# A hybrid encoder layer on one core: router logits from rows ahead of their norm, and the first tokens' branches inside the attention loop

## The chip, the cores and the metric

The kernel runs on one core of one Trainium2 chip as one program. The metric is the device time of one execution in microseconds; the number that counts is the median of several executions on the chip. Engines are named as in the profile: PE (TensorE matmul), PEld (its weight load), DVE (VectorE), ACT (ScalarE), POOL (GpSimd), SP (the queue that issues most DMAs).

## What is computed

One layer on 2048 tokens of width 1024, in float32. Cut to what matters here:

```python
h   = rmsnorm(x, norm1_g);  proj = h @ w_in          # RWKV columns | attention columns | two gates
y_rwkv = rwkv7_branch(...) @ w_rwkv_out              # group norm of the scan's output, bonus, gate
y_attn = dilated_attention_branch(...) @ w_attn_out  # 3 dilations, merged by their softmax sums
gates  = sigmoid(gate_logits)
x   = x + (gates[:, :, 0] * y_rwkv + gates[:, :, 1] * y_attn) @ w_out
h2  = rmsnorm(x, norm2_g)                            # x * rsqrt(mean(x * x) + eps) * norm2_g
grp_logits = h2 @ w_router_group  + b_router_group   # 4 groups, the best is taken
exp_logits = h2 @ w_router_expert + b_router_expert  # 32 experts, 2 of the 8 in that group
moe = sum over the two experts of  weight * ((silu(h2 @ w_gate[e]) * (h2 @ w_up[e])) @ w_down[e])
out = x + moe
```

## The kernel before

The program is one long unrolled sequence. Products that must be exact in float32 are made from a rounded part and the rest of it (`wh[:, 0]` and `wh[:, 1]`, the rest being "raw minus rounded", a subtraction), in three passes each.

1. *Projection, scan, dense products* (to about 1793 us). They leave the scan's output `y_d`, queries, keys and values `qkv_d` and gates `g_d` in DRAM.
2. *Attention* (lines 893 to 973): dilation groups `g` = 2, 1, 0, each with 16 windows of 128 tokens; group 0 goes by pairs of windows. A window transposes its q/k rows into PSUM under the tag `tq` (two buffers, L909), makes scores (L938, L940), exponentials (L947), transposes them (L953), multiplies with the values (L963) and stores `ob` to `o_d`. `parts_of_weights` loads and splits the weights of the next stage in between. Memory of this stage is the pool `at` and the PSUM pool `psC`; `stC.close()` (L1046) frees both.
3. *Preparation of the first 256 tokens*: constants (L975 to L987), then `rwkv(0, psC, "tq")` (L997): it loads the scan's output, norms it by head on DVE, adds the bonus on POOL (L1030, L1031), multiplies with the gate product (L1036, L1037) and turns the result with `split_T` (L988) into `YT[0]`. After `stC.close()` the pools `y5` and `psE` open, and `attn(0)` (L1124) loads the three groups' outputs `oc`, weights and adds them on DVE (L1133 to L1149) and turns them into `OT[0]`.
4. *Eight blocks `q` of 256 tokens* (L1223): eight calls of `merge` (gated sums, L1166 to L1173, with gates `tg` loaded at L1160 and L1161), then per tile `j` of 128 tokens two calls of `residual` (L1182, tag `px`). `norm2` (L1186) stores the row, squares it on ACT, takes the root on DVE (`rsqrt`, L105 to L110, small operations), and makes `h2` (L1194). `logits` (L1198) transposes `h2` (tag `th`, L1204), copies it on ACT (L1206) and multiplies with `wr` (L1209); L1212 adds the biases. `route` (L1064) picks group and experts on DVE, counts ranks with two matmuls (L1100, L1101, tag `pl`), and at last places tokens (L1117 to L1122). The odd tile's logits and the route of block `q` are a generator, `late`, that is advanced in block `q + 1`; so are `attn(q + 1)` and `rwkv(q + 1)`, as `nA` and `nR`, in block `q`. PSUM of this stage: `ab`, `t5` and `px` with two buffers each, `pl` and `th` with one.
5. *End of the route* (L1256 to L1279): experts are ordered by their counts; a matmul makes the tables `IDX1`, `IDX2`, `EOF` and the weights. `load_gu(0, G)` loads the first expert's weights and splits them (L1296 on ACT, L1297 with `eng`, here POOL).
6. *32 experts in that order*: rows fetched by POOL's indirect DMA (L1386), products (L1426, L1431, L1470), results added to the output by indirect DMA.

The order of instructions on each engine, and of DMAs on SP, is not that of the source. A planner orders them at build time: it takes what its own model finds ready, the earlier place in the source first, and gives out the buffers of each tag in that order. At run time every engine and queue is strictly in order. A pool's memory can be written when the last user of what lay there is done; the constants' pool `w5` and `yb`, and later the experts' `rw` and `sw`, lie on the same side of the memory.

## Time and profile before

| | us |
|---|---|
| median of 3 executions (lowest, highest) | 3318.16 (3314.29, 3323.53) |
| the profiled execution | 3319.97 |
| its span, first to last instruction | 3318.2 |
| PE / PEld / DVE / ACT / POOL busy, share of span | 91% / 74% / 67% / 46% / 17% |
| attention, first transposes to last output | 1793.5 to 2047.7 |
| from there to the first residual product | to 2086.0 |
| eight blocks, to the last residual product | to 2511.1 |
| route and first rows, to the first expert's first product | to 2556.9 |
| experts | to 3318.2 |

How to read the rows below. A row of a table by stretches gives the stretch, its length, then for PE, PEld, DVE, ACT and POOL the busy time in us and the number of instructions in it, then the granted TensorE clock as a share of full speed, the DMA engines' busy share and GB/s. A row of waits gives the engine, what it was about to do and its line, "<-" what it waited for, then the us in total, how often, and the longest. A row of the timeline gives start in us, duration of the merged group in us, engine, line, operation, written tile "<-" read tiles, shapes and the number of instructions; in brackets the idle time of that engine ahead of it and what ended it. A matmul of float32 takes two passes and shows as such in the durations.

### The profile page before, as it was taken

How to read it: one execution, taken by the hardware profiler on the slowest of the kernel's cores; microseconds unless marked ns; L12 is line 12 of the kernel's file. 1: busy time of each engine (PE TensorE's matmuls, PEld its weight loads, DVE VectorE, ACT ScalarE, POOL GpSimd, SP SyncE). 2: the span in 40 equal slices, each digit the busy share in tenths (PEclk: the TensorE clock that was granted, in tenths of full speed). 3: DMA queues.
4: the chain of work that ended last, by engine and by line, in shares of the span. 5: the costliest groups of instructions: out<-in, count | busy, mean ns of one | idle time of the engine just before them, and what ended most of it. 6: DMA issues, size and time to landing. Idle time of an engine off the chain costs nothing. (4 is left out here: it accounts for less than half of the span.)

```text
span 3318.2 us, 71986 instructions
## 1 busy us (share of the span) xinstructions
PE 3009.8 (91%) x29005; PEld 2449.2 (74%) x29005; DVE 2219.4 (67%) x4149; ACT 1538.3 (46%) x2946; POOL 563.3 (17%) x648
## 2 busy tenths in 40 slices
PE   6999978888989989998999987999996999999997
PEld 4788777668867787678877986877784667777775
DVE  6433367576867686749664876668764677788885
ACT  6633344453343434443524864111112666777764
POOL 0000012020202121202110001324233111222231
PEclk9999988999989999999999998999997999999998
DMA  7244365666545654554556554444333889999996
GB/s 277 80 124 147 112 223 182 216 206 201 159 150 187 196 181 147 172 187 156 167 175 192 177 171 140 127 137 135 129 114 124 295 298 333 339 336 340 328 308 198
DMA packets 361242, 652.75 MB, mean 197 GB/s; under 512 B 33741, under 2 KB 181917, under 8 KB 356674
## 3 DMA queue, kind: packets, MB, share of 16 engines
q1 hardware_dynamic: 338698, 599.74, 54.1%
q0 software_dynamic: 11104, 36.32, 4.4%
q10 hardware_dynamic: 11104, 12.06, 1.2%
q8 instruction: 229, 3.75, 0.5%
q14 instruction: 107, 0.88, 0.1%
HBM read 497.59 MB, written 153.16 MB: 196 GB/s over the span
## 5 line engine op out<-in xcount | busy, mean ns | idle before, releaser
L1297 DVE TENSOR_TENSOR wh<-raw,wh 128x1024 fp32r<-128x1024 f32 x376 | 442.4, 1221 | 78.6 <-ACT wh L1296 78.2
L724 PE MATMUL dn<-wh,hk 128*128 128x256 f32 x3456 | 472.4, 294 | 19.3 <-DVE wh L667 5.5
L724 PEld LDWEIGHTS dn<-wh,hk 128*128 128x128 f32 x3456 | 441.0, 198 | 38.5 <-issue 10.6
L1296 ACT ACTIVATE wh<-raw 128x1024 fp32r<-128x1024 f32 x384 | 387.0, 1053 | 140.6 <-DMA raw<-in_w_down_dram 61.0
L728 PE MATMUL dn<-hk,wh 128*128 128x512 f32 x1536 | 406.0, 412 | 27.2 <-DVE wh L667 10.1
L1426 PE MATMUL pgu<-wh,xT 128*128 128x512 f32 x1536 | 375.1, 401 | 0.2 <-ACT xT L1401 0.2
L728 PEld LDWEIGHTS dn<-hk,wh 128*128 128x128 f32 x1536 | 286.9, 194 | 103.3 <-ACT gs L738 12.1
L1426 PEld LDWEIGHTS pgu<-wh,xT 128*128 128x128 f32 x1536 | 286.1, 189 | 77.4 <-issue 6.1
L282 PE MATMUL pp<-hq,wh 128*128 128x512 f32 x1008 | 248.7, 399 | 1.4 <-ACT hq L218 1.1
L282 PEld LDWEIGHTS pp<-hq,wh 128*128 128x128 f32 x1008 | 188.1, 189 | 47.1 <-ACT hq L218 1.8
L1182 PE MATMUL px<-w,mT 128*128 128x512 f32 x768 | 198.7, 410 | 0.0
L1470 PE MATMUL py<-wh,hT 128*128 128x512 f32 x768 | 191.3, 401 | 0.5 <-ACT hT L1448 0.5
L484 POOL TENSOR_TENSOR t<-t,ld 128x512 f32<-128x512 f32 x32 | 53.7, 1677 | 806.9 <-DVE t L473 525.3
L1182 PEld LDWEIGHTS px<-w,mT 128*128 128x128 f32 x768 | 144.6, 191 | 37.3 <-issue 3.4
L1470 PEld LDWEIGHTS py<-wh,hT 128*128 128x128 f32 x768 | 140.4, 188 | 33.1 <-issue 1.2
L1362 POOL DMA_INDIRECT out_dram<-ys,IDX x49 | 102.5, 2092 | 303.7 <-issue 93.9
L738 ACT ACTIVATE gs<-dn,drv 128x512 f32<-128x512 f32 x64 | 75.8, 1184 | 128.4 <-PE dn L728 101.8
L1166 PE MATMUL ab<-yT,w 128*128 128x256 f32 x768 | 113.6, 292 | 7.5 <-DVE tg L1169 3.9
L1386 POOL DMA_INDIRECT xg<-h_d,IDX x49 | 73.0, 1489 | 276.8 <-PE tx L1400 155.8
L285 ACT ACTIVATE u<-pp 128x512 f32<-128x512 f32 x56 | 61.2, 1094 | 123.8 <-PE pp L282 98.6
L1166 PEld LDWEIGHTS ab<-yT,w 128*128 128x128 f32 x768 | 98.6, 191 | 12.9 <-DVE tg L1169 6.1
L423 ACT ACTIVATE uv<-pre 32x512 f32<-32x512 f32 x128 | 75.2, 588 | 59.6 <-PE pre L417 58.4
(416 smaller groups left out, 5454.8 us busy)
## 6 DMA issues: line engine op xcount, KB each, us to landing
wh<-wc_d SPq DMA_DIRECT2D x204, 512.0 KB
raw<-in_w_gate_dram SPq DMA_DIRECT2D x64, 1024.0 KB
raw<-in_w_up_dram SPq DMA_DIRECT2D x64, 1024.0 KB
raw<-in_w_down_dram SPq DMA_DIRECT2D x64, 1024.0 KB
wc_d<-wh SPq DMA_DIRECT2D x68, 512.0 KB
ld<-rkk_d SPq DMA_DIRECT2D x192, 128.0 KB
raw<-in_w_in_dram SPq DMA_DIRECT2D x82, 256.0 KB
g_d<-gs SPq DMA_DIRECT2D x64, 256.0 KB
```

The costliest lines, as they stand in the source:

```text
L282: PE.matmul(pp, whs[k // 4][:, a, k % 4], hq[q][k // 2][:, k % 2, b], start=n == 0, stop=n == 3 * KT - 1)
L423: S.activation(uv[p * 64:p * 64 + 32, s::2].rearrange("p s (h e n) -> p s h e n", e=2, n=N)[:, :, :, e], pa[o:o + 32], AF.Copy)
L724: PE.matmul(pp[e][:, j * 256:(j + 1) * 256], lhs(2 * e + j, hk, k, a), wk_[:, b], start=k + j + m == 0, stop=k + j + m == KT + 2, skip_gro ...
L728: PE.matmul(pp[e], wk_[:, a, e * 128:e * 128 + 128], hk[k // 2][:, k % 2, b], start=k + m == 0, stop=k + m == KT + 1)
L738: S.activation(natural(gs), by_residue(pp[e]), AF.Tanh, scale=0.5, bias=DP[:, 38 + ct:39 + ct])
L1166: PE.matmul(pa[:, e], wt[k][:, a, cs_], src[:, k, b], start=e + n == 0, stop=n == 3 * nk - 1, skip_group_check=True)
L1182: PE.matmul(px, mT[k // 4][:, k % 4, a, j * 128:(j + 1) * 128], wO[k][:, b, fs], start=n == 0, stop=n == 3 * KT - 1)
L1296: S.activation(wh[:, 0, ks], raw[:, ks], AF.Copy)
L1297: eng.tensor_tensor(wh[:, 1, ks], raw[:, ks], wh[:, 0, ks], op=OP.subtract)
L1362: G.indirect_dma_start(out=x2_d, out_offset=bass.IndirectOffsetOnAxis(ap=idx, axis=0), in_=src, in_offset=None, bounds_check=T - 1, oob_is ...
L1426: PE.matmul(pgu[n], xT[:, x_, 4 * a + k], wh[:, w_, k], start=a + k + m == 0, stop=a + k + m == 6)
L1470: PE.matmul(py[f], hT[:, x_, 2 * a + k], wh[:, w_, k, f * 512:(f + 1) * 512], start=a + k + m == 0, stop=a + k + m == 4)
```

## The change

Four things are done.

- The constants' loads, `split_T` and `rwkv` stand ahead of the attention loop. `wr` is multiplied with `norm2_g` (`g2T`) once. A new generator `attn0` makes the weighted sum of the first two tiles in buffers of `yb` (tags `y0`, `y1`, and small ones). `early`, the chain of `rwkv(0)` and `attn0`, is advanced once per window of group 0 from window 8 on. What is left behind `stC.close()` is `turn_o(0)`, the transposes and their split.
- `norm2` returns the root `r2`; `logits` transposes `xr` itself and puts `r2` into its last operation. Both halves are transposed and copied first (tag `t5`, two buffers; `th` is gone), then the 16 matmuls follow; `pl` has two buffers.
- `late` is advanced at other places: transposes of the odd tile after merge 3, its logit matmuls and the first part of the route after merge 7 and ahead of the residual, the ranks behind `residual(xr[0], mT, 0, 1)` as before, the placing of tokens behind the last residual. At the end the experts' order is worked out ahead of the last placing, in other buffers.
- `load_gu(0)` splits the first expert's weights on DVE, not POOL.

```diff
+    wr = mk(w5, [128, KT, 36], F32, "wr")
+    nc.sync.dma_start(wr[:, :, 0:4], w_router_group[0].rearrange("(k p) e -> p k e", p=128))
+    nc.sync.dma_start(wr[:, :, 4:36], w_router_expert[0].rearrange("(k p) e -> p k e", p=128))
+    g2T = mk(yb, [128, KT], F32, "bsum")
+    nc.sync.dma_start(g2T, norm2_g[0].rearrange("(k p) -> p k", p=128))
+    V.tensor_tensor(wr, wr, g2T[:, :, None].to_broadcast([128, KT, 36]), op=OP.mult)
...
+    def attn0():
+
+        for j in range(2):
+            oc = mk(yb, [128, 3, 264], F32, f"y{j}")
+            for g in range(3):
+                nc.sync.dma_start(oc[:, g], o_d[g, j * 128:(j + 1) * 128])
+            OC.append(oc)
+            yield
+            nm, sm = oc[:, :, 256:260], oc[:, :, 260:264]
...
+            V.tensor_tensor(og, og, wg[:, :, :, None].to_broadcast([128, 3, 4, N]), op=OP.mult)
+            V.tensor_tensor(oc[:, 0, 0:256], oc[:, 0, 0:256], oc[:, 1, 0:256], op=OP.add)
+            V.tensor_tensor(oc[:, 0, 0:256], oc[:, 0, 0:256], oc[:, 2, 0:256], op=OP.add)
+            yield
...
+                if g == 0 and i >= 7:
+                    next(early, None)
+                    if i == 7:
+                        early = chain(rwkv(0, psC, "tq"), attn0())
...
-    for _ in rwkv(0, psC, "tq"):
+    for _ in early:
         pass
 
     stC.close()
...
-        pr = mk(psE, [128, 2, 2, NE], F32, "pl", bufs=1)
+        pr = mk(psE, [128, 2, 2, NE], F32, "pl")
...
-        pk2 = mk(psE, [2 * NE, CAP], F32, "pl", bufs=1)
+        pk2 = mk(psE, [2 * NE, CAP], F32, "pl")
...
+    def turn_o(q, src):
+
+        OT[q] = mk(y5, [128, 2, 2, 256], F32R, "oT")
+        split_T(OT[q], src, 2, psE, "t5")
...
-        return h2
-
-    def logits(h2, lg):
-        pl = mk(psE, [128, 36], F32, "pl", bufs=1)
+        return r2
+
+    def logits(xr, r2, lg):
+
+        xT = []
         for k4 in range(2):
-            pt = mk(psE, [128, 4, 128], F32, "th", bufs=1)
+            pt = mk(psE, [128, 4, 128], F32, "t5")
             for k in range(4):
                 kk = k4 * 4 + k
-                PE.transpose(pt[:, k], h2[:, kk * 128:(kk + 1) * 128], ident)
-            hT = mk(y5, [128, 4, 128], F32, "h2T", bufs=2)
-            S.activation(hT, pt, AF.Copy)
-            for k in range(4):
-                kk = k4 * 4 + k
-                PE.matmul(pl, hT[:, k], wr[:, kk], start=kk == 0, stop=kk == KT - 1)
-            if k4 == 0:
-                yield
-        V.tensor_tensor(lg, pl, br, op=OP.add)
-
-    def tail(q, LG, h2):
-
-        yield from logits(h2, LG[:, 1])
+                PE.transpose(pt[:, k], xr[:, kk * 128:(kk + 1) * 128], ident)
+            xT.append(mk(y5, [128, 4, 128], F32, "h2T", bufs=2))
+            S.activation(xT[k4], pt, AF.Copy)
+        yield
+        pl = mk(psE, [128, 36], F32, "pl")
+        for kk in range(KT):
+            PE.matmul(pl, xT[kk // 4][:, kk % 4], wr[:, kk], start=kk == 0, stop=kk == KT - 1)
+        V.scalar_tensor_tensor(lg, pl, r2, br, op0=OP.mult, op1=OP.add)
+
+    def tail(q, LG, xr, r2):
+
+        yield from logits(xr, r2, LG[:, 1])
         yield
         yield from route(q, LG)
 
-    for _ in attn(0):
-        pass
+    turn_o(0, [oc[:, 0, 0:256] for oc in OC])
...
             merge(q, ct, mT)
-            if ct in (1, 3, 5):
+            if ct == 3:
                 next(late, None)
+
+        next(late, None)
+        next(late, None)
...
-        h2 = norm2(2 * q, xr[0])
+        r2 = norm2(2 * q, xr[0])
         next(nA, None)
         residual(xr[1], mT, 1, 0)
-        for _ in late:
-            pass
-        for _ in logits(h2, LG[:, 0]):
+        for _ in logits(xr[0], r2, LG[:, 0]):
             pass
         next(nA, None)
         residual(xr[1], mT, 1, 1)
-        for _ in chain(nA, nR):
+        for _ in chain(late, nA, nR):
             pass
-        late = tail(q, LG, norm2(2 * q + 1, xr[1]))
-    for _ in late:
-        pass
-
-    key = mk(y5, [2 * NE, NE], F32, "tm")
+        late = tail(q, LG, xr[1], norm2(2 * q + 1, xr[1]))
+    for _ in range(4):
+        next(late)
+
+    key = mk(y5, [2 * NE, NE], F32, "h2T", bufs=2)
...
     V.tensor_scalar(order, byrank, rnk, None, op0=OP.is_equal)
+    for _ in late:
+        pass
...
-            eng.tensor_tensor(wh[:, 1, ks], raw[:, ks], wh[:, 0, ks], op=OP.subtract)
+            V.tensor_tensor(wh[:, 1, ks], raw[:, ks], wh[:, 0, ks], op=OP.subtract)
...
-    wgu = load_gu(0, G)
+    wgu = load_gu(0)
```

## Rows read from the trace of the kernel before

**Rows 1.** Table by stretches, busy times: the stages and blocks named in the prediction.

```profile
2050.00:2064.50 14.50, 3.04 (x21) 2.44 (x19) 10.61 (x30) 1.53 (x3) 0.00 (x0) 0.65 0.78 250
2194.85:2256.62 61.77, 57.18 (x320) 48.10 (x319) 43.14 (x130) 11.13 (x26) 19.24 (x19) 0.92 0.39 127
2256.62:2313.66 57.04, 52.47 (x321) 44.26 (x320) 43.11 (x130) 11.14 (x26) 18.97 (x19) 1.00 0.44 138
2530.80:2546.40 15.60, 4.59 (x14) 2.18 (x14) 12.04 (x22) 7.16 (x8) 9.28 (x4) 0.50 0.41 152
2600.00:3318.20 718.20, 691.57 (x4064) 501.89 (x4062) 555.95 (x598) 471.74 (x574) 165.16 (x89) 0.98 0.92 311
```

**Rows 2.** Timeline, PE and SP at the start of the attention.

```profile
1793.49 1.09 PE L909 MATMUL tq<-ident,qkr 128*128 128x128 f32 x8 [3.81 <-ACT gs L738]
1797.02 0.34 SPq L976 DMA_DIRECT2D gnB<-in_gn_w_dram  x1
```

**Rows 3.** Timeline, from the attention's end to the first residual product.

```profile
2048.81 3.12 PE L1166 MATMUL ab<-yT,w 128*128 128x256 f32 x24 [1.10 <-DVE yT L995]
...
2051.05 0.47 SPq L1160 DMA_DIRECT2D tg<-g_d  x1
...
2063.35 1.11 PE L993 MATMUL t<-ident,oc 128*128 128x128 f32 x4 [11.43 <-DVE oc L1149]
...
2086.02 11.39 PE L1182 MATMUL px<-w,mT 128*128 128x512 f32 x48
```

**Rows 4.** Table by stretches, ten microseconds within group 0 of the attention.

```profile
2020.00:2030.00 10.00, 9.45 (x76) 8.15 (x75) 7.00 (x11) 5.14 (x18) 0.00 (x0) 1.00 0.40 108
```

**Rows 5.** Timeline, POOL's two operations of `rwkv(0)`.

```profile
2038.93 1.91 POOL L1030 TENSOR_TENSOR y<-y,bsum 128x1024 f32<-128x1024 f32 x1 [255.54 <-DVE bsum L1029]
...
2040.91 2.36 POOL L1031 TENSOR_TENSOR y<-y,y 128x1024 f32<-128x1024 f32 x1
```

**Rows 6.** Waits of PE from 2080 to 2512 us, the blocks.

```profile
PE pl L1209 <- ACT h2T L1206: 8.8, 13, 0.9
PE th L1204 <- DVE h L1194: 8.7, 6, 1.5
...
PE pl L1121 <- DVE OW L1117: 1.3, 6, 0.2
```

**Rows 7.** Timeline, from the last residual to the first expert's product.

```profile
2511.10 0.69 DVE L1184 SCALAR_TENSOR_TENSOR xr<-px,xr 128x512 f32<-128x512 f32 x1 [4.56 <-PE px L1182]
...
2515.31 1.28 DVE L1194 SCALAR_TENSOR_TENSOR h<-xr,r,g 128x1024 f32<-128x1024 f32 x1
...
2524.11 0.20 DVE L1212 TENSOR_TENSOR LG<-pl,br 128x36 f32<-128x36 f32 x1 [7.51 <-PE pl L1209]
2524.33 0.38 SPq L1292 DMA_DIRECT2D raw<-in_w_gate_dram  x1
...
2529.95 2.00 ACT L1296 ACTIVATE wh<-raw 128x1024 fp32r<-128x1024 f32 x2 [1.85 <-PE pl L1101]
...
2546.25 0.19 DVE L1272 TENSOR_SCALAR IDX<-t 128x32 int32<-128x32 f32 x1 [1.37 <-PE t L1271]
```

**Rows 8.** Timeline, DVE beside POOL's split of the first weights.

```profile
2530.71 0.35 DVE L1109 TENSOR_TENSOR tm<-OH,pk 128x64 f32<-128x64 f32 x2
2531.08 9.28 POOL L1297 TENSOR_TENSOR wh<-raw,wh 128x1024 fp32r<-128x1024 f32 x4 [43.09 <-DVE tm L1109]
...
2531.42 4.40 DVE L1109 TENSOR_TENSOR tm<-OH,io 128x64 f32<-128x64 f32 x2
```

**Rows 9.** Timeline, POOL's fetches of rows beside DVE's splits of weights.

```profile
2558.50 1.56 DVE L1297 TENSOR_TENSOR wh<-raw,wh 128x1024 fp32r<-128x1024 f32 x1 [0.25 <-ACT wh L1296]
...
2559.13 1.77 POOL L1386 DMA_INDIRECT xg<-h_d,IDX  x1 [0.16 <-issue]
...
2560.46 1.23 DVE L1297 TENSOR_TENSOR wh<-raw,wh 128x1024 fp32r<-128x1024 f32 x1 [0.39 <-ACT wh L1296]
...
2562.77 0.95 POOL L1386 DMA_INDIRECT xg<-h_d,IDX  x1 [0.30 <-issue]
```

More of the change, by code (lines that the diff above doesn't have):

```diff
@@ L890, in hybrid_layer_kernel @@
     made = 0
+    gnB = mk(w5, [128, 2, HD], F32, "gnB")
+    nc.sync.dma_start(gnB[:, 0], gn_w[0:1, :].to_broadcast([128, HD]))
+    nc.sync.dma_start(gnB[:, 1], gn_b[0:1, :].to_broadcast([128, HD]))
+    g2 = mk(w5, [128, D], F32, "g2")
+    nc.sync.dma_start(g2, norm2_g[0:1, :].to_broadcast([128, D]))
+    gup = mk(w5, [128, HD], F32, "gup")
+    nc.sync.dma_start(gup, g_up[0])
+    wr = mk(w5, [128, KT, 36], F32, "wr")
+    nc.sync.dma_start(wr[:, :, 0:4], w_router_group[0].rearrange("(k p) e -> p k e", p=128))
@@ new lines, in attn0 @@
+    def attn0():
+        for j in range(2):
+            oc = mk(yb, [128, 3, 264], F32, f"y{j}")
+            for g in range(3):
+                nc.sync.dma_start(oc[:, g], o_d[g, j * 128:(j + 1) * 128])
+            OC.append(oc)
+            yield
+            nm, sm = oc[:, :, 256:260], oc[:, :, 260:264]
+            mn = mk(yb, [128, 4], F32, "ri5")
+            V.tensor_tensor(mn, nm[:, 0], nm[:, 1], op=OP.min)
+            V.tensor_tensor(mn, mn, nm[:, 2], op=OP.min)
+            wg = mk(yb, [128, 3, 4], F32, "mu")
+            V.tensor_tensor(wg, mn[:, None, :].to_broadcast([128, 3, 4]), nm, op=OP.subtract)
+            S.activation(wg, wg, AF.Exp)
+            V.tensor_tensor(sm, sm, wg, op=OP.mult)
+            den = mk(yb, [128, 4], F32, "bsum")
+            V.tensor_tensor(den, sm[:, 0], sm[:, 1], op=OP.add)
+            V.tensor_tensor(den, den, sm[:, 2], op=OP.add)
+            V.reciprocal(den, den)
+            V.tensor_tensor(wg, wg, den[:, None, :].to_broadcast([128, 3, 4]), op=OP.mult)
+            og = oc[:, :, 0:256].rearrange("p g (h n) -> p g h n", n=N)
+            V.tensor_tensor(og, og, wg[:, :, :, None].to_broadcast([128, 3, 4, N]), op=OP.mult)
+            V.tensor_tensor(oc[:, 0, 0:256], oc[:, 0, 0:256], oc[:, 1, 0:256], op=OP.add)
+            V.tensor_tensor(oc[:, 0, 0:256], oc[:, 0, 0:256], oc[:, 2, 0:256], op=OP.add)
+            yield
@@ L891, in hybrid_layer_kernel @@
+    YT, OT, OC = {}, {}, []
     wA, wB, wO = [], [], []
     parts_of_weights = weights()
+    early = iter(())
     for g in (2, 1, 0):
@@ L1042, in hybrid_layer_kernel @@
-    YT, OT = {}, {}
-    for _ in rwkv(0, psC, "tq"):
+    for _ in early:
         pass
@@ L1150, in attn @@
         yield
-        oT = OT[q] = mk(y5, [128, 2, 2, 256], F32R, "oT")
-        split_T(oT, oc[:, :, 0, 0:256], 2, psE, "t5")
+        turn_o(q, [oc[:, j, 0, 0:256] for j in range(2)])
+    def turn_o(q, src):
+        OT[q] = mk(y5, [128, 2, 2, 256], F32R, "oT")
+        split_T(OT[q], src, 2, psE, "t5")
     def merge(q, ct, mT):
@@ L1296, in piece, with load_gu @@
             S.activation(wh[:, 0, ks], raw[:, ks], AF.Copy)
[L1297 removed]
+            V.tensor_tensor(wh[:, 1, ks], raw[:, ks], wh[:, 0, ks], op=OP.subtract)
         return raw, wh
[L1300 to L1301 removed]
+    def load_gu(e):
+        return [piece(w, e, a, 4, 512) for a in range(2) for w in (w_gate, w_up)]
     def load_dn(e):
         return [piece(w_down, e, a, 2, 1024) for a in range(2)]
[L1306 removed]
+    wgu = load_gu(0)
     def overflow_list():
```

121 lines of the change are left out of this document (53 added, 68 removed).

## Prediction

> **What bounds the kernel now.** Three views were read. The first is the busy table by stretches. The experts' stage, from 2600 to the end, keeps the DMA engines 0.92 busy and streams weights [rows 1]; its first loads that depend on the routing wait for the route, so it is shifted by whatever the stages ahead of it gain, and the diff does not touch it otherwise. Of the stretches ahead, two have an idle TensorE at a low clock: 2050 to 2064.5, with 3.04 us of PE work in 14.5 us, and 2530.8 to 2546.4, with 4.59 us in 15.6 us at the granted clock 0.50 (1.2 GHz) [rows 1]. In between, a block of 256 tokens takes 57.04 us with 52.47 us of PE work [rows 1]: PE sets its length, so only PE's own waits can be won there. The second view is the waits of PE, which names them; the third is the timeline around both idle stretches, which says what ended each wait. Source order is not machine order here: a planner issues what its own model finds ready. The load of `gnB` stands behind the attention loop in the source and was issued at 1797.02, at its start [rows 2]. So I count on dependences that change, not on places of lines.
>
> **Part 1: the first 256 tokens' branches.** Before, `rwkv(0)` was finished at the end of the attention, and the merges' first half ran from 2048.81. Then PE sat 11.43 us until the attention branch of the first 256 tokens had been loaded, weighted and added, at 2063.35; the first `px` matmul came at 2086.02 [rows 3]. From first merge to first `px` that is 37.2 us. After, the weighted sum lies inside the attention stage, in buffers of `yb`, and only four transposes and their split are left behind `stC.close()`. The eight merges are 8 x 18 = 144 matmuls; 24 took 3.12 us [rows 3], so 18.7 us. Next late are the gate loads `tg`: they were issued from 2051.05 on [rows 3], behind the loads of `oc`, which are gone from that place, and the third merge needs the first of them. I give 1.5 us for that and for the split: 20.2 us instead of 37.2, a gain of 17. What the step adds lies in the attention stage: some ten short DVE operations and three large ones per tile, two `Exp`, six loads on SP. There PE was busy 9.45 of 10 us [rows 4], so DVE work is covered by PE work. The PE work of `rwkv(0)` (its transposes and two gate products) moves from the draining end into that full stretch, and its two gate products hold both `tq` buffers of PSUM while POOL does 1.91 + 2.36 us for them [rows 5]; the transposes of the next q/k rows need the same two buffers. The loop makes them one pair of windows ahead, so most of this is hidden; without that cover it costs the 4.3 us and some DVE work. The nine loads of constants and the product of `wr` with `g2T` move ahead of the attention's loads in the source. SP's queue is in order, but PE's first attention transposes waited 3.81 us for the last gate eviction of the stage before, at 1793.49, and a load takes about 0.35 us to issue [rows 2]; nine of them are 3 us, in front of loads that have that time. The 4-byte reads of `g2T` have no row like them; I bound them between 0 and 3.81 us of DVE delay at that place and take 0, since no q/k work could start earlier anyway. I take 2 us for the attention stage in all (bounds 0 and 8). Sum of part 1: -15 us, bounds -19 and -8.
>
> **Part 2: logits from rows not yet normed, in the blocks.** The gain `norm2_g` goes into `wr` once, the factor `r2` into the last operation on DVE. So the transposes need `xr`, not `h2`. PE waited 8.7 us in six blocks for `h2` [rows 6], the length of the chain of square, root and scaling. The odd tile's copies and its logit matmuls are now four merges apart, and the even tile's transposes are issued as a pair; both answer the 8.8 us in 13 waits for `h2T` [rows 6]. With the last ranks moved behind the residual the 1.3 us for `OW` [rows 6] go too. That is 18.8 us at most. The number of matmuls and transposes stays. New waits: the transposes share `t5` with the gate products of `rwkv(q + 1)`, whose two buffers come free only after POOL's 4.3 us and two DVE products; and eight DVE operations of the last ranks now fall where the splits of the next block's branches need DVE. On PE's path I charge 1 us a block for these, 7 us: -12 us. The bounds are -23.5 and -5: the upper end is all waits plus the 4.7 us by which one block was longer at clock 0.92 than at 1.00 [rows 1], the lower end is 2 us of new waits in each of seven blocks. The two `next` of the logits and the route run ahead of the residual: the route's DVE chain then overlaps the products of `rwkv(q + 1)` on DVE, and PE needs its result only 11 us of residual matmuls later.
>
> **Part 3: the last tile, the route and the first expert.** After the last residual, at 2511.10 + 0.69, the chain was: root and `h2` (to 2516.6), transposes, copies and matmuls in two rounds, logits at 2524.11 [rows 7]. After, transposes and copies run while the root is worked out. The last operation needs both `r2` and the products; `h2` itself (1.28 us) lies ahead of it on DVE, so the logits come just behind 2516.6: -7.5 us. The first weights are loaded when the constants' memory comes free with the logits, so they move too. Then the route runs 6.5 us as before. In the following 15.6 us to the table of tokens (2546.25) DVE was slowed: with POOL splitting the first weights for 9.28 us, one pair of L1109 took 4.40 us, where the pair ahead of it had taken 0.35 us [rows 7, 8]. This split is now on DVE. Without the slowing the chain is about 9 us: its DVE work, three returns from PE at the low clock, and the ordering of experts, which no longer waits for the last ranks. But eight splits of 1.23 us [rows 9] are queued on the same engine. From the issue of the first weights to ACT's first split were 5.6 us [rows 7]; so splits are ready just when the chain waits for PE, and each that is put in a gap of PE delays the chain by what it overhangs, at most 1.23 us. I charge 2 us: 11 instead of 15.6, -4.5 us. The bounds are -6.5 (no overhang) and +3 (six splits in line ahead of the table). Sum of part 3: -12 us, bounds -14 and -4.5.
>
> *A rule against this part.* Rows first: the fetch of the experts' rows by POOL took 1.77 us beside a DVE split and 0.95 us without [rows 9]. The Trainium skill, "SBUF — State Buffer", section "SBUF: two separate sides", says that a DMA which GpSimd issues needs GpSimd to write its descriptors, and that some DVE operations lock it out of a shared port for their whole length. By that rule, moving the splits to DVE puts them against the first two fetches; this trace agrees with 0.8 us on one. By it the sum would be 1 to 2 us less.
>
> **Sum.** -15 - 12 - 12 = -39 us. The profiled execution took 3319.97 us, 1.8 us more than its span; the median of the three runs is 3318.16. From the profiled one 3281, from the median 3279. The block with the low clock may belong to that execution alone, so I go from the median and say 3279 us. All lower bounds together give -17.5 (3301), all upper ones -56.5 (3262).
>
> **The rivals.**
> (a) *The attention stage takes it back.* `tq` is held by the gate products at POOL's pace, the next q/k transposes come late, and in a stage with PE at 9.45 of 10 every stall counts; the added loads delay the start too. Against it: transposes are made a pair of windows ahead. Price: the 8 us bound and the same again for the clock, part 1 shrinks to 0: 3294.
> (b) *The blocks gain nothing:* waits for `h2` and `h2T` turn into waits for a `t5` buffer. For it: POOL's 4.3 us and two buffers. Against it: before, the gate products were consumed well before the even tile's transposes. Time: 3291.
> (c) *The splits on DVE sit in front of the route.* The planner puts them where its model has the weights landed; if they land later, DVE waits with the chain behind it. Part 3 keeps only its 4.5 us: 3287.
> (d) *The planner already had it.* It hoists `rwkv(0)` in the old source as far as buffers allow, so part 1's move might change no order. Against it: `oc` lived in a pool that opens only after the attention. Without part 1's gain: 3294, as in (a).
> (e) *Slower.* The even tile's transposes stand in PE's order ahead of the last residual matmuls, and behind a `t5` buffer that the gate products hold until POOL has finished. If the planner's model has POOL done 6 us too early, PE stops for 6 us in every block. Price: 7 x 6 = 42 us and 4.7 us for each block that drops to the low clock, 33 more, against -39: 3354. It decides from 5.6 us of new waits a block. Speaking against it: POOL starts these two as soon as the bonus is there, and a residual half of 24 matmuls lies between.
> (f) *All waits go, and the low-clock block with them:* 3262.
>
> **How the numbers follow.** Forecast 0.58, (a) and (d) together 0.13, (b) 0.11, (c) 0.08, (f) 0.07, (e) 0.03. The range is 3258 to 3302: it takes in (a), (b), (c), (d), (f) and the bounds, and leaves out (e) and the misses of more than one part, about 0.15. A measurement of this kernel can tell about 0.3% (10 us) from no change. Faster by more than that, below 3308: 0.92. Within: 0.05, when two of (a), (b), (c) meet. Slower: 0.03.
>
> **What would show it.** Part 1: the first `px` about 20 us behind the last attention output instead of 37, no wait of PE for `oc`. Part 2: no wait for `h2` or `h2T`, blocks near 55 us. Part 3: the last logits 5 us behind the last residual instead of 13, 9 to 12 us from ranks to table. Wrong would be: transposes of q/k waiting for `tq`, PE waiting for POOL's or DVE's products in a block, or DVE standing on a split while the route is behind it.

## The result

| | before | after |
|---|---|---|
| median of 6 executions (lowest, highest), us | 3319.9 (3311.8, 3323.5) | 3296.8 (3284.6, 3304.5) |
| the profiled execution, us | 3319.97 | 3284.64 |
| its span, us | 3318.2 | 3282.9 |

The ratio of the medians is 0.9933, with a 95% interval from 0.9918 to 0.9948: faster by 23 us, where 39 us were forecast; 3296.8 lies inside the range. The profiled pair differs by 35.3 us, because the profiled execution of after is the fastest of its six. One of six executions of r2_neither below took 4135.6 us, at a granted clock of 0.65; its median is that of the other five. Two more profiles of the same kernel, from the runs below, stand beside it. The stages were cut at events that every kernel has: first scores of the attention, start of its 41st output tile `ob` (of 48; the first tokens' branches are interleaved from there on), end of the last `ob`, first `px`, first `px` of the second block, last residual addition, last `LG`, first `IDX`, first product of the experts, end.

| stage, us | before | after | again (r1) | again (r11) |
|---|---|---|---|---|
| to the attention's first scores | 1795.1 | 1793.8 | 1793.1 | 1799.3 |
| to the 41st `ob` | 210.1 | 213.2 | 212.2 | 212.5 |
| to the end of the last `ob` | 42.5 | 52.9 | 54.2 | 51.3 |
| to the first `px` | 38.3 | 24.2 | 24.2 | 25.3 |
| to the second block's first `px` | 51.8 | 53.5 | 55.3 | 54.7 |
| to the last residual | 374.0 | 355.3 | 355.4 | 355.2 |
| to the last `LG` | 12.5 | 5.5 | 5.5 | 5.5 |
| to `IDX` | 22.0 | 13.7 | 13.7 | 13.7 |
| to the experts' first product | 10.6 | 10.7 | 11.5 | 11.1 |
| to the end | 761.3 | 760.0 | 760.3 | 762.9 |

From the second block on, the three executions agree to 0.2 us a stage up to `IDX`. What differs from run to run lies ahead of the change (1793 to 1804 us to the first scores in the profiles of all kernels here), in the attention and, by up to 3 us, in the first block and the experts.

### The profile page after: what moved, and what is told of

Same layout as the page of the kernel before. It is cut to its first block, busy times and chain, and to the rows that moved or that the text cites. A ratio compares the mean times of both kernels' runs of the same rounds, so it can differ in the third digit from the quotient of the medians.

```text
span 3282.9 us, 72016 instructions
## 1 busy us (share of the span) xinstructions
PE 3003.9 (92%) x29005; PEld 2446.4 (75%) x29005; DVE 2229.6 (68%) x4168; ACT 1538.7 (47%) x2947; POOL 539.3 (16%) x640
## 5 line engine op out<-in xcount | busy, mean ns | idle before, releaser
L1340 DVE TENSOR_TENSOR wh<-raw,wh 128x1024 fp32r<-128x1024 f32 x384 | 450.8, 1218 | 80.0 <-ACT wh L1339 79.0
L728 PE MATMUL dn<-hk,wh 128*128 128x512 f32 x1536 | 408.8, 415 | 28.3 <-DVE wh L667 11.6
L282 PEld LDWEIGHTS pp<-hq,wh 128*128 128x128 f32 x1008 | 188.0, 188 | 47.1 <-ACT hq L218 1.8
L1405 POOL DMA_INDIRECT out_dram<-ys,IDX x49 | 91.4, 1865 | 311.5 <-issue 111.4
L1206 PEld LDWEIGHTS ab<-yT,w 128*128 128x128 f32 x768 | 97.8, 191 | 16.3 <-DVE tg L1209 12.5
```

The lines of the kernel that those rows point to most:

```text
L282: PE.matmul(pp, whs[k // 4][:, a, k % 4], hq[q][k // 2][:, k % 2, b], start=n == 0, stop=n == 3 * KT - 1)
L728: PE.matmul(pp[e], wk_[:, a, e * 128:e * 128 + 128], hk[k // 2][:, k % 2, b], start=k + m == 0, stop=k + m == KT + 1)
L1206: PE.matmul(pa[:, e], wt[k][:, a, cs_], src[:, k, b], start=e + n == 0, stop=n == 3 * nk - 1, skip_group_check=True)
L1340: V.tensor_tensor(wh[:, 1, ks], raw[:, ks], wh[:, 0, ks], op=OP.subtract)
L1405: G.indirect_dma_start(out=x2_d, out_offset=bass.IndirectOffsetOnAxis(ap=idx, axis=0), in_=src, in_offset=None, bounds_check=T - 1, oob_is ...
```

## The profile after

The table by stretches (columns as in [rows 1]): two rows of before that its section did not have, then after.

```profile
2005.20:2047.69 42.49, 39.44 (x302) 33.40 (x300) 24.61 (x38) 24.24 (x80) 4.26 (x2) 1.00 0.38 110
2047.69:2086.02 38.33, 23.68 (x154) 20.91 (x153) 29.08 (x57) 5.20 (x13) 15.03 (x14) 0.78 0.56 170
```

```profile
2007.00:2059.94 52.94, 45.03 (x302) 37.58 (x300) 30.54 (x62) 25.53 (x83) 4.27 (x2) 0.90 0.31 94
2050.00:2060.00 10.00, 8.96 (x41) 8.29 (x41) 0.69 (x1) 3.12 (x11) 0.00 (x0) 0.50 0.04 14
2059.94:2084.15 24.21, 22.24 (x155) 20.23 (x156) 17.23 (x28) 3.81 (x8) 10.40 (x12) 0.93 0.75 236
2247.89:2302.89 55.00, 52.38 (x320) 44.09 (x320) 45.91 (x130) 11.20 (x26) 19.45 (x19) 1.00 0.45 143
2504.86:2512.16 7.30, 4.36 (x14) 2.30 (x14) 6.76 (x25) 5.41 (x6) 0.00 (x0) 0.50 1.03 382
```

The last eight tiles of the attention hold the same 302 PE instructions in both kernels. PE is busy 39.44 us with them before and 45.03 after, because the granted clock fell from 1.00 to 0.90, and idle 7.9 us instead of 3.0. In the last ten microseconds the clock is 0.50, the lower level (1.2 GHz). A block takes 55.0 us against 57.04 in [rows 1], with the same PE work: 2.6 us of idle time, not 4.6. The stretch from the ranks to the table, the last row, takes 7.3 us instead of the 15.6 in [rows 1], with the same 14 PE instructions and the clock at 0.50 in both.

The timeline of PE where [rows 3] showed the end of the attention:

```profile
2055.84 3.68 PE L1063 MATMUL po<-v,tb 128*128 128x64 f32 x16 [0.57 <-DVE tb L1058]
2059.99 1.11 PE L913 MATMUL t<-ident,y 128*128 128x128 f32 x4 [0.47 <-ACT ob L1065]
2060.76 3.60 PE L1206 MATMUL ab<-yT,w 128*128 128x256 f32 x18
...
2081.91 1.68 PE L1206 MATMUL ab<-yT,w 128*128 128x256 f32 x12 [1.82 <-DVE tg L1209]
...
2084.15 5.13 PE L1222 MATMUL px<-w,mT 128*128 128x512 f32 x21
```

The wait of 11.43 us for `oc` in [rows 3] is gone; the merges run into the first `px` with one wait of 1.8 us. But this begins at 2060, not at 2048. The waits of PE in the blocks, where [rows 6] named `h`, `h2T` and `OW`:

```profile
PE ab L1206 <- DVE tg L1209: 6.1, 11, 0.8
PE t L913 <- DVE oT L915: 6.0, 7, 0.9
PE px L1222 <- POOL mT L1213: 2.4, 6, 0.4
```

All three names are gone. What PE waits for now are gated sums (`tg`), splits of the branches (`oT`) and POOL's half of `mT`. From the second block on these are 5.7, 5.2 and 2.4 us, where the kernel before had 2.0, 4.8 and none: the wait for `oT` is hardly new. The tail, where [rows 7] and [rows 8] showed it:

```profile
2492.26 0.69 DVE L1224 SCALAR_TENSOR_TENSOR xr<-px,xr 128x512 f32<-128x512 f32 x1 [4.96 <-PE px L1222]
...
2497.02 1.28 DVE L1235 SCALAR_TENSOR_TENSOR h<-xr,r,g 128x1024 f32<-128x1024 f32 x1
2498.23 0.25 DVE L1253 SCALAR_TENSOR_TENSOR LG<-pl,r,br 128x36 f32<-128x36 f32 x1
...
2505.57 0.36 DVE L1145 TENSOR_TENSOR tm<-OH,io 128x64 f32<-128x64 f32 x2
...
2506.84 1.21 DVE L1340 TENSOR_TENSOR wh<-raw,wh 128x1024 fp32r<-128x1024 f32 x1
...
2512.16 0.19 DVE L1315 TENSOR_SCALAR IDX<-t 128x32 int32<-128x32 f32 x1 [0.23 <-PE t L1314]
```

`LG` stands right behind `h`, as the sum had it. The pair of L1145 takes 0.36 us (4.40 in [rows 8]), and only three splits of 1.21 us, of which one is shown, lie ahead of `IDX`.

## The experiments: the first tokens' branches

Theory at this point: the early branches save what was forecast behind the attention and lose it inside, so part 1 nets nothing. Four kernels ran side by side.

**r1_same**, no edit.

> The changed kernel once more, unaltered, to see what repeats. In its profile of record the last output tile of the attention (the last ob) is done at 2059.6 us (before: 2047.3), the first px begins at 2084.2 (2086.0), the blocks from the first px to the last take 408.2 us (425.1), the last xr to the expert list IDX1 19.9 (35.1), and the expert stage from its first product 760.0 (761.4). If the loss in the attention is work and waits, 2059.6 returns within 1 us and the first px within 2. Times between 3284 and 3305 us are expected, as its other executions gave; a stage that is longer than in the profile of record by 5 us or more then names what the profiled execution had better than the others, and I expect it as a stretch of lower granted clock outside the stages that the change touches.

Measured: 3292.5 us, ratio 0.9924 [0.9906, 0.9943]. Last `ob` at 2059.6, first `px` at 2083.8: the loss in the attention repeats to 0.4 us (1.7 us less in r11). The spread is not one stretch: its attention had less clock than the profile after (0.84 against 0.90 in the last eight tiles), and in r11 it is the stages ahead that are 5.5 us longer.

**r2_neither**

```diff
-                if g == 0 and i >= 7:
-                    next(early, None)
-                    if i == 7:
-                        early = chain(rwkv(0, psC, "tq"), attn0())
...
-    for _ in early:
+    for _ in rwkv(0, psC, "tq"):
...
-    turn_o(0, [oc[:, 0, 0:256] for oc in OC])
+    for _ in attn(0):
+        pass
```

> The changed kernel with the first 256 tokens' branches put back: no part of them between the attention's windows, the RWKV branch behind the last window, the attention branch behind that in a buffer of the block stage, as in the kernel before. The logits, the ranks and the splits of the first expert stay changed. Theory (what the early branches gain for the first merges is paid back in the attention, part 1 nets about 2 us): last ob at 2046 to 2047, first px at 2084 to 2086, the whole within 3 us of the changed kernel in the same rounds, 0.989 to 0.996 of the kernel before. Rival (part 1 is worth its forecast 15 us, and the profile of record had an unlucky stage): first px at 2097 or more against the changed kernel, 12 to 15 us longer.

Measured: 3292.9 us, 0.9919 [0.9898, 0.9940]; the changed kernel beside it 3292.5, 0.9924. The medians differ by 0.4 us and the ratios by 1.7 us in the opposite direction: part 1 is worth nothing that can be told, and not 15. The absolute times expected for this profile were missed (last `ob` 2055.9, first `px` 2095.0), since its attention lost 7 us ahead of the 41st tile. By stages it is the kernel before again: 43.0 and 39.2 us.

**r4_rwkv_only**

```diff
-                        early = chain(rwkv(0, psC, "tq"), attn0())
+                        early = rwkv(0, psC, "tq")
...
-    turn_o(0, [oc[:, 0, 0:256] for oc in OC])
+    for _ in attn(0):
+        pass
```

> The other half: only the RWKV branch of the first 256 tokens between the windows, as in the changed kernel; the attention branch behind the attention in a buffer of the block stage, as in the kernel before. Theory (the RWKV branch is what lengthens the attention): last ob at 2056 to 2060, behind it the wait for oc as before, first px at 2094 to 2099, the whole 8 to 14 us longer than with neither branch early. Rival (the attention branch is what lengthens it): last ob at 2047 to 2050, first px at 2084 to 2088, the whole within 3 us of the kernel with neither.

Measured: 3303.8 us, 0.9956 [0.9941, 0.9971], 10.9 us longer than with neither branch early, as the theory had it (its last `ob` came at 2072.5, 12 later than expected, with the clock at 0.77).

**r3_attn_only** (the output `OT[0]` gets the staging buffers of the weights, which move from `at` to `yb`)

```diff
-                raws.append(mk(at, [128, 512], F32, "wst", bufs=2))
+                raws.append(mk(yb, [128, 512], F32, "wst", bufs=2))
...
+        yield from turn_o(0, [oc[:, 0, 0:256] for oc in OC], psC, "tq")
...
-                if g == 0 and i >= 7:
+                if g == 0 and i >= 3:
                     next(early, None)
-                    if i == 7:
-                        early = chain(rwkv(0, psC, "tq"), attn0())
+                    if i == 3:
+                        early = attn0()
...
-    for _ in early:
+    for _ in chain(early, rwkv(0, psC, "tq")):
```

> Of the first 256 tokens only the attention branch is worked out early: its loads from the fourth window on, its normalisation in the windows behind, its transposes and their splits into a buffer of its own still inside the attention; the RWKV branch stands behind the last window, as in the kernel before. Theory (what lengthened the attention is the RWKV branch: its transposes and products stop TensorE between the windows, and behind the last window its work is missing as filling): last ob at 2046 to 2050, no wait of the merges for oc (11.4 us before), first px at 2068 to 2074, the whole 10 to 16 us shorter than with neither branch early and than the changed kernel. Rival (any VectorE work and loads between the windows cost it, the attention branch's too): last ob at 2054 or later, first px at 2078 or later, the whole within 5 us of the changed kernel.

Measured: 3293.2 us, 0.9928 [0.9909, 0.9946]: the expected 10 to 16 us did not come. The waits of PE from 2055 to 2142 us name one reason, an accident of this edit: the last weights were queued behind `OT[0]` in the shared buffers.

```profile
PE px L1226 <- ACT w L881: 3.3, 1, 3.3
PE px L1226 <- DVE w L882: 1.3, 1, 1.3
```

The tables by stretches of r1, r2, r4 and r3, from the 41st `ob` to the end of the last, in this order:

```profile
2005.42:2059.59 54.17, 47.10 (x302) 40.20 (x299) 30.55 (x62) 25.61 (x83) 4.27 (x2) 0.84 0.31 90
```

```profile
2012.90:2055.85 42.95, 39.45 (x302) 33.39 (x300) 24.59 (x38) 24.27 (x80) 4.26 (x2) 1.00 0.38 109
```

```profile
2014.10:2072.49 58.39, 49.88 (x303) 43.02 (x300) 35.44 (x60) 26.40 (x82) 4.26 (x2) 0.77 0.32 98
```

```profile
2011.70:2058.25 46.55, 40.01 (x306) 33.86 (x304) 34.98 (x60) 25.81 (x82) 4.26 (x2) 1.00 0.42 119
```

The PE instructions are the same to within 4. With `rwkv(0)` at the end (r2, r3) the clock stays at 1.00; with `rwkv(0)` pulled forward (r1, r4) it falls, and PE needs 4 to 10 us more for the same work (43.7 us in r11, 45.0 in after, 47.1 in r1, 49.9 in r4, against 39.4). All kernels here fall in line: the mean clock of these eight tiles is 1.00 in the five profiles with `rwkv(0)` at the end and 0.77 to 0.92 in the nine with it early. The timeline of r2 shows how the end is filled: transposes of `rwkv(0)` lie between the last products, and 16 products take 2.00 us; in after they take 3.68.

```profile
2052.80 0.55 PE L913 MATMUL tq<-ident,y 128*128 128x128 f32 x3
2053.43 2.00 PE L1063 MATMUL po<-v,tb 128*128 128x64 f32 x16
```

Cut once more at the start of the 46th `ob`, the eight tiles tell where the time goes: before, after and r11, each in two rows.

```profile
2005.20:2034.56 29.36, 27.40 (x218) 23.88 (x217) 16.83 (x26) 17.31 (x57) 0.00 (x0) 1.00 0.44 127
2034.56:2047.69 13.13, 12.05 (x86) 9.53 (x85) 7.78 (x12) 6.93 (x24) 4.26 (x2) 1.00 0.25 72
```

```profile
2007.00:2043.35 36.35, 31.30 (x232) 25.80 (x231) 23.41 (x53) 19.15 (x62) 4.27 (x2) 1.00 0.44 129
2043.35:2059.94 16.59, 13.73 (x72) 11.78 (x71) 7.14 (x10) 6.38 (x21) 0.00 (x0) 0.70 0.05 16
```

```profile
2011.84:2049.85 38.01, 33.72 (x232) 28.56 (x231) 23.41 (x53) 19.26 (x62) 4.26 (x2) 0.91 0.42 123
2049.85:2063.09 13.24, 9.98 (x72) 8.04 (x71) 7.14 (x10) 6.38 (x21) 0.00 (x0) 0.96 0.06 21
```

The 14 PE instructions of `rwkv(0)` move from the second part to the first (86 to 72, 218 to 232); they are 3.8 us of PE time before and 4.1 in after. The end does not get shorter by losing them: it takes 13.1 us before, 13.2 in r11 and, at the lower clock, 16.6 in after. The first part gets longer by more than they take: by 7.0 us in after, by 8.6 in r11. Among the rest is a new wait of `rwkv(0)`'s own transposes for the product on DVE behind POOL's two operations, the same in after, r1, r4 and r11:

```profile
PE tq L913 <- DVE y L957: 1.6, 2, 1.3
```

In r1, r11 and r4 the clock is at 0.50 for 6.8, 6.8 and 13.7 us from 1 to 2 us behind this wait; in after it is not. So the place of `rwkv(0)` is shown to cost the clock, but not which gap lowers it, and r11 had 1.00 up to 2062 us with the end unfilled.

**r5_attn_weights** and **r12_attn_weights** (the same kernel twice) mend r3's accident:

```diff
                 if g < 2:
                     next(parts_of_weights, None)
+                if g == 1 and i % 2:
+                    next(parts_of_weights, None)
```

> The attention branch alone early, as in r3_attn_only, but with the output weights' pieces loaded and split a little faster (a second piece behind every other window of the second pass), so that all are done before the branch's output takes their staging buffer. In r3 the first px waited 4.6 us for two pieces of these weights, which stood behind that output. Theory (the attention branch costs the windows 4 us, without a drop of the granted clock, and saves 14 to 16 us behind them; what hid the gain in r3 was the weights): no px waits for w, the first block back from 58.9 us to 53 to 55, from the 41st output tile to the second block's first px 122 to 126 us (133.7 with neither branch early, 130.7 and 133.7 with both), the whole 6 to 10 us under the changed kernel. Rival (a first px that begins earlier only waits for the second token group's branches): the first block still at 57 us or more, the whole within 3 us of the changed kernel.

> The changed kernel unaltered, for the kernel beside it in these rounds: 0.990 to 0.995 of the kernel before, from the 41st output tile to the second block's first px 130 to 134 us, from there to the last xr 355 to 356, from there to the end 790 to 792.

> r5_attn_weights once more, beside the changed kernel in the same rounds. Its stretch from the 41st output tile to the second block's first px took 125.1 us against 130.7 and 133.7; its time did not show that gain. Theory (the stage's gain is real, and the profile of r5 lost it before the 41st tile to a lower granted clock, as other kernels' profiles did too): the stretch again at 122 to 127 us, the whole 4 to 9 us shorter than r11_same. Rival (the weights moved into the second pass and the branch's work in the third take back what the stage gains): the stretch from the attention's first scores to the 41st output tile 4 us or more above r11's and the whole within 3 us of it.

Measured: r5 3296.0 us, 0.9925 [0.9903, 0.9947]; r12 3292.6, 0.9915 [0.9895, 0.9935], beside r11, the changed kernel, with 3297.1, 0.9918 [0.9902, 0.9933]. From the 41st `ob` to the second block r5 takes 125.1 and r12 124.2 us, r11 131.3: the stage's gain is real, and no `px` waits for `w`. But from the first scores to the 41st `ob` r5 and r12 took 221.3 and 220.5 us, the profiles of the changed kernel 212 to 213: the sign that r12's rival named. Other kernels, whose program differs little up to there, show 212 to 221 as well, so both the moved weights and chance may be in it. Whether this version beats the changed kernel stays open: the intervals overlap.

## The experiments: blocks and tail

**r6_pool_split**

```diff
-    wgu = load_gu(0)
+    wgu = load_gu(0, G)
```

> The changed kernel with one thing put back: the low halves of the first expert's gate and up weights are split on GpSimd, as before. In the changed kernel the odd tile's logits to the expert list take 13.7 to 14.0 us (22.1 before), of which my forecast gave 4.05 to VectorE not being held beside a GpSimd split. Theory: that stretch rises by 3 to 5 us, to 17 to 19, the step from the list to the expert's first product stays at 10 to 12, the whole 3 to 5 us longer than the changed kernel. Rival (the 8 us come from the ranks' new place and the split's engine is hidden): the stretch within 1 us of 13.9, the whole within 2 us.

Measured: 3304.5 us, 0.9940 [0.9919, 0.9962]. From `LG` to `IDX` 17.45 us, 3.8 more than with the splits on DVE, as the theory had it. Its expert stage took 768.5 us, 6 to 9 more than in the changed kernel's profiles; POOL still splits at its beginning, but it did so in the kernel before as well, whose stage took 761.3 us; from one profile the cause is open. The timeline shows how two small operations stand for the length of a split each:

```profile
2517.18 4.69 POOL L1340 TENSOR_TENSOR wh<-raw,wh 128x1024 fp32r<-128x1024 f32 x2 [37.90 <-ACT wh L1339]
2517.26 2.33 DVE L1301 TENSOR_TENSOR h2T<-h2T,idn 64x32 f32<-64x32 f32 x1
2519.52 2.47 DVE L1156 TENSOR_SCALAR rr<-io,RK 128x192 f32<-128x192 f32 x1
```

The same two operations take 0.18 and 0.30 us in the changed kernel. The Trainium skill, "SBUF — State Buffer", section "SBUF: two separate sides", calls the port pair that DVE and GpSimd share an exclusive lock and not a split of bandwidth: what starts first has it for its whole instruction. The two rows agree, each with one POOL split of 4.69 / 2 us.

**r7_normed** undoes the logits' source, **r8_order** the places of `late`, and **r10_tags_only** both (r7 and r10 also drop the product of `wr` with `g2T`):

```diff
-        return r2
+        return h2
...
-        for _ in logits(xr[0], r2, LG[:, 0]):
+        for _ in logits(h2, LG[:, 0]):
```

```diff
-            if ct == 3:
+            if ct in (1, 3, 5):
                 next(late, None)
-        next(late, None)
-        next(late, None)
...
         residual(xr[1], mT, 1, 0)
+        for _ in late:
+            pass
...
-        for _ in chain(late, nA, nR):
+        for _ in chain(nA, nR):
```

> The changed kernel with the logits worked out from the normed rows again (transposes of h2, the weights not scaled, no factor behind the product); the order, the buffers and the early branches stay changed. Theory (the waits for h2 and h2T were what the blocks lost, and the tail waits for the whole normalisation): the last xr to LG back from 5.5 to 12 to 13 us; waits of the transposes for h2 return in the blocks; from the second block's first px to the last xr 355.3 us becomes 364 to 372; the whole 14 to 24 us longer. Rival (the blocks gained by their new order and second buffers, the rows not normed matter in the tail alone): the blocks within 3 us of 355.3, the whole 6 to 9 us longer.

> The changed kernel with the old places of the odd tile's logits, choice and ranks in the next block: a step behind the second, fourth and sixth merge and the rest ahead of the even tile's logits, where the changed kernel has one behind the fourth, two behind the merges and the rest at the block's end. Rows not normed, second buffers and the tail stay changed. Theory: only the small waits of the ranks' products (1.3 us for OW in the kernel before, in six waits) and some of the even logits' come back: from the second block's first px to the last xr 355.3 us becomes 356 to 360, the whole 0 to 5 us longer. Rival (the order is what gained in the blocks): 364 us or more, the whole 9 us or more longer.

> Of the block's edits only the PSUM buffers are left: the logits again from the normed rows and the odd tile's steps again at their old places, so r7_normed and r8_order together; tail's table and early branches stay changed. r7 alone took 379.9 us from the second block's first px to the last xr, r8 alone 397.8, the changed kernel 355.3, the kernel before 374.0 with one block of low clock (4.7 us of it). Theory (the two edits belong together: rows not normed are early enough only if the ranks don't stand ahead of them, and the old order is harmless only where the logits wait for the norm anyway): 366 to 374 us, shorter than either alone. Rival (sharing t5 is what costs r7 and r8, and the changed kernel escapes it): 385 us or more, as r8 or worse.

**r9_old_tags** keeps both edits and undoes only the PSUM buffers:

```diff
-            pt = mk(psE, [128, 4, 128], F32, "t5")
+            pt = mk(psE, [128, 4, 128], F32, "th", bufs=1)
...
-        pl = mk(psE, [128, 36], F32, "pl")
+        pl = mk(psE, [128, 36], F32, "pl", bufs=1)
```

(and `bufs=1` for the two other tiles with the tag `pl`)

> The changed kernel with the PSUM buffers of the logits and the ranks as before: the logits' transposes in one bank of their own (th) and not in the two that the branches' transposes use (t5), the product, the sums of ranks and the table in one bank (pl) and not two. Order, rows not normed, tail and early branches stay changed. From the second block's first px to the last xr the changed kernel takes 355.3 us. Theory (two tiles' logits and ranks at once in a block need the second bank): the second half of each tile's transposes waits for ScalarE's copy of the first, 0.6 to 0.9 us twice a block, 363 to 372 us, the whole 8 to 17 us longer. Rival (the banks don't matter, order and rows alone do): within 3 us of 355.3.

| kernel | time, us | ratio | second block to last residual, us |
|---|---|---|---|
| both edits, new PSUM buffers (r1, r11) | 3292.5, 3297.1 | 0.9924, 0.9918 | 355.4, 355.2 |
| rows normed, new order (r7) | 3332.1 | 1.0026 [1.0010, 1.0043] | 379.9 |
| rows not normed, old order (r8) | 3342.0 | 1.0066 [1.0044, 1.0089] | 397.8 |
| neither, new buffers, the halves' transposes still a pair (r10) | 3322.8 | 1.0007 [0.9996, 1.0019] | 363.3 |
| both edits, old buffers (r9) | 3280.4 | 0.9881 [0.9865, 0.9897] | 343.7 |
| neither, old buffers (before) | 3319.9 | | 374.0 |

r7 and r8 came out above what the theory expected, and in r8 the rival (the order) was right: each edit without the other makes the kernel slower than before. r10 is 3 us under its expectation and shorter than either, so the two do belong together. r10 also parts the gain of the blocks. 4.7 us of the 374.0 before are its block at the lower clock [rows 1]. Of the 14 us left, 6 come with r10, which has no wait for `h2T` any more but still 8.8 us for `h`; the two edits together bring only the other 8. How much of the 6 is the pairing of the halves no run tells. r9 went the other way than either theory said: the old buffers are better by 11.6 us in the blocks and by 16.7 us in the whole, and the interval lies clear of the changed kernel's beside it, [0.9902, 0.9933] in r11. It is the fastest version, and it beats both kernels, in one round of five executions.

*Why r8 loses 42 us.* The waits of PE in its blocks, and one block's timeline on DVE, then PE:

```profile
PE pl L1157 <- DVE OW L1153: 10.5, 6, 1.8
PE ab L1206 <- DVE tg L1209: 8.2, 7, 1.4
PE px L1222 <- ACT mT L1212: 8.2, 6, 1.4
```

```profile
2355.54 1.28 DVE L1235 SCALAR_TENSOR_TENSOR h<-xr,r,g 128x1024 f32<-128x1024 f32 x1
2356.74 0.68 DVE L1224 SCALAR_TENSOR_TENSOR xr<-px,xr 128x512 f32<-128x512 f32 x1
2357.34 0.31 DVE L1156 TENSOR_SCALAR rr<-io,RK 128x192 f32<-128x192 f32 x1
2357.57 0.35 DVE L1153 TENSOR_TENSOR OW<-OH,TW 128x64 f32<-128x64 f32 x2
```

```profile
2355.35 0.87 PE L1246 MATMUL t<-ident,xr 128*128 128x128 f32 x6
2357.97 0.86 PE L1157 MATMUL pl<-rr,OW 128*64 128x192 f32 x4 [1.75 <-DVE OW L1153]
```

The logits no longer need `h`, but the ranks' products that stand among them in PE's order need `OW`, and DVE works `h` and the residual off first. In the changed kernel these products come behind the last residual, where they find `OW` ready. This wait explains why the rows not normed gain nothing with the old order: r10, with r8's order on PE, waits 8.8 us for `h` and 1.3 for `OW` in the same place. What r8 loses against r10, 34.5 us, is something else: 12.0 us of waits for `mT` (ACT's 8.2 above and 3.8 for POOL), of which r10 has none, and 21.5 us more of PE time for the same work. Only one of r8's six full blocks behind the first ran at 1.00, and took 59.0 us; the others, of 61.0 to 63.2 us, had a granted clock of 0.92 to 0.97. Why `mT` comes late was followed in one block: the last gated sum starts 3.4 us behind the first `px` on DVE, and 1.8 us behind it in r10. r7 keeps the transposes' wait for `h`, 13.6 us in six blocks (8.7 in [rows 6]); two of its blocks, of 62.3 and 61.1 us, were at a clock of 0.92 and 0.94, the others took 58.0 or less.

*Why r9 gains.* Its waits of PE in the blocks, a block in the table by stretches, and the turn from one block to the next on PE:

```profile
PE ab L1206 <- DVE tg L1209: 5.6, 6, 1.1
PE t L913 <- DVE oT L915: 3.0, 6, 0.5
```

```profile
2306.70:2359.80 53.10, 51.72 (x321) 44.03 (x320) 44.95 (x130) 11.52 (x26) 19.23 (x19) 1.00 0.46 147
```

```profile
2335.82 0.38 PE L1246 MATMUL th<-ident,xr 128*128 128x128 f32 x2
...
2337.86 0.41 PE L913 MATMUL t<-ident,y 128*128 128x128 f32 x2 [0.50 <-DVE oT L915]
2338.11 0.44 PE L1246 MATMUL th<-ident,xr 128*128 128x128 f32 x2
```

With a bank of their own the odd tile's transposes are put into the turn, among the branches' transposes, where PE waits for splits. With `t5` shared they come ten microseconds later, among the merges. These two rows of r1 show the turn and the place:

```profile
2336.32 0.74 PE L913 MATMUL t<-ident,y 128*128 128x128 f32 x4 [0.86 <-DVE oT L915]
...
2346.68 1.04 PE L1246 MATMUL t<-ident,xr 128*128 128x128 f32 x8
```

r9 has no wait for `mT` at the residual (2.4 us in six blocks after), 3.0 us of waits for `oT` instead of 5.2 in the same seven blocks of r1, and 0.7 us less PE time a block. No PE wait names a `t5` buffer. So the shared tag seems to cost through the order that the planner can make, not through a stall that carries its name; this is read from the rows, and no run changed the order alone. `th` and `pl` were not put back one at a time, so the share of each is open, and so is where the whole gains 5 us more than the blocks.

## Why the prediction was right and where it failed

*The sum.* Faster, inside the range; 18 us above the forecast. The profiled pair gives -35.3, but the three profiled executions of after lie 4 to 12 us under the medians of their rounds, so the medians' -23 stands. Where the other executions lose these microseconds no trace shows. That the profiled pair comes within 4 us of the forecast is luck: part 1 fell short by 15 us, and 4.7 us of the block at the lower clock before, 3 us in part 3 and 2 in part 2 stand against that.

*Part 1, forecast -15, measured about 0: the term that failed.* "A gain of 17" behind the attention was mechanically right: 38.3 became 24.2 us, 14.1 won; the missing 3 are the first merges at the low clock and one wait for `tg`. The failing step is "I take 2 us for the attention stage (bounds 0 and 8)", which rested on "DVE work is covered by PE work" with PE at 9.45 of 10 us [rows 4]. The last eight tiles alone took 9 to 12 us more, outside the bounds. I named the PE work of `rwkv(0)` ("moves from the draining end into that full stretch") and gave its PE time no price, neither where it arrives nor where it leaves. Where it arrives PE had no room: its 4.1 us are paid in full, and PE's waits, in r1, r4 and r11 also the lower clock, add 3 to 6.5 us. Where it leaves nothing is won: the end takes 13 to 18 us without it and 13.1 with it. r2, r3 and r4 show that it is this branch: the clock goes with the place of `rwkv(0)`, and the attention branch alone costs 3 to 4 us in these tiles at clock 1.00 (what it costs ahead of them is less than the 7 us by which profiles differ there). A second step was missing: the next tokens' branches move from the wait into the first block, which is 1.7 to 3.5 us longer; DVE is busy 37.5 us in it, 29.6 before.

*Rival (a)* came true in size (its "8 us and the same again for the clock"); its mechanism only in part. No transpose of q/k rows waits for a `tq` buffer; what waits is `rwkv(0)`'s own transposes, at POOL's pace, for 1.6 us where (a) had 4.3. The clock did take as much again: of r1's extra 11.7 us 7.7 are PE time at the lower clock, which lasts for 6.8 us from just behind this wait and for 10.4 us at the end. (d) falls: with neither branch early the wait for `oc` is back (11.7 us in r2).

*Part 2, forecast -12.* The profiled pair gives -18.7 from the second block on, 4.7 of it the low-clock block of before, and +1.7 in the first block, which stands under part 1. That is -14: right in size. Right too: the waits for `h`, `h2T` and `OW` went. The charge of 7 us for new waits met 6.5 us of them from the second block on (`tg` +3.7, `mT` +2.4, `oT` +0.4), but none for a `t5` buffer behind POOL, the first of its two reasons, and only the 0.4 for the splits, the second: that it fits is luck. What sharing `t5` costs came by another way, and r9 prices the new buffers at 11.6 us. Wrong was the sentence that I count on dependences and not on places of lines. r8 changes places alone and costs 42 us; that this is the 7 x 6 us of rival (e) is chance, since nearly half of it is PE time at the lower clock and none of its waits is (e)'s. The gain is not a sum of edits: each of the two alone is a loss.

*Part 3, forecast -12, measured -15.2.* Logits -7.0 (forecast -7.5). From logits to table -8.3, where -4.5 was forecast with a best case of -6.5. The 2 us for overhanging splits was too much: `IDX` waits 0.23 us for PE, not for the split ahead of it, and from the ranks to the table it is 7.3 us where 11 were forecast. Of the 15.2, r7 takes back 6.9 when the rows are normed, r6 3.8 with POOL's splits; if these add, 4.5 remain for what was not undone by itself, above all the experts' order ahead of the last ranks. Rival (c) did not occur.

*The rule against part 3* (the Trainium skill's page named there) would have cost 1 to 2 us. The fetches did meet DVE's splits, but from `IDX` to the experts' first product it is 10.7 us against 10.6: no such loss shows. The rule speaks of some DVE operations; that these splits are among them I took from one fetch of 1.77 us. Beside the five splits that follow `IDX` in after, three fetches took 0.87, 0.95 and 1.91 us.

## What to carry to other kernels

Work at the draining end of a stage may be free filling. Before pulling it forward, price it in full where it arrives, with its own waits, and price the end that is left without it at its old length and at the lower clock. When an edit removes a dependence, ask which instruction stands next in the engine's order and what it needs: here it paid only with the old neighbour moved as well. A second use of a rotating buffer can cost time even where no wait names it; try the separate buffer.

## What the runs showed of the hardware

In after the granted clock is 1.00 up to 2048 us and 0.50 from 2050 on; between 2046 and 2050 PE was idle for 1.9 us, most of it in two pieces of 0.92 and 0.78 us. It came back after 2062, and PE was 8.96 of 10 us busy from 2050 on. I had not expected that gaps so short are followed by 12 us at the lower clock. In r11 the same two pieces, ending at 2053.69 and 2056.39, are followed by 1.00 up to 2062, so they alone do not decide. And in r6 an addition of 32 x 1 numbers on DVE took 5.16 us beside two POOL splits of together 4.64 us. It started ahead of them, while POOL was at a fetch of rows, and ended with the second; why it lay through both is not shown.

```profile
2528.41 1.19 POOL L1429 DMA_INDIRECT xg<-h_d,IDX  x1 [6.54 <-issue]
2529.14 5.16 DVE L1359 TENSOR_TENSOR cap<-cap,cp 32x1 f32<-32x1 f32 x1
2529.64 4.64 POOL L1340 TENSOR_TENSOR wh<-raw,wh 128x1024 fp32r<-128x1024 f32 x2
```
